# Expert stage of a fused encoder block: a third place for arriving weights, low parts only on VectorE, the last 16 tokens' gates on VectorE, gathers requested a step later

## Chip, core and metric

One core of a Trainium2 chip runs the whole program in one launch. The metric is the device time of that core in microseconds. The engines are TensorE (PE: matmuls, PEld: weight loads beside them), VectorE (DVE), ScalarE (ACT), GpSimd (Pool) and SyncE (SP, which here only issues DMAs). Each engine takes its instructions in program order, so one that waits holds all that stand behind it on its engine.

## What is computed

An encoder block over 512 tokens of width 2048: adaLN, neighbourhood attention and a bidirectional RWKV-7 mixer in parallel, an output projection, and then a product-key expert layer, which is where the change lies. Each token selects 16 of 16,384 single-neuron experts in each of 8 heads:

```
def chunk(args):
    xc, ec, gc = args
    hidden = jax.nn.gelu(jnp.einsum('cd,chkd->chk', xc, exp_u[ec]), approximate=False) * gc
    return jnp.einsum('chk,chkd->cd', hidden, exp_v[ec])
```

All of it is float32. A product x·w is made of three matmuls on parts: x and w are each split into a high part in a shorter format and a low part that holds the rest, and high·high, high·low and low·high are summed.

## The kernel before

The 512 tokens are handled in two ways. For the first 144 (TS) the rows of the selected experts are gathered: class Picks fetches, for one pick of 128 tokens, 128 rows of 8 KB by an indirect DMA that Pool issues (L1231), and DVE takes a dot product with it (L1253) or adds it, scaled, into y3 (L1264). k.rb = 3 row places go round. The other 368 tokens (TD) go through all experts densely, with a gate that is zero for experts that were not selected.

The dense part is class Experts. A unit "u" computes the hidden values of 128 experts for 368 tokens, a unit "v" adds 4 such experts' groups (512 experts) into 256 of the 2048 output columns. Each unit has two steps; a step needs one weight part of 128x1024 floats (512 KB, tile raw) and does 24 matmuls of 368 columns. There are 512 steps in all. form() runs the first 64 while the gates are still being made; main() runs the other 448, and is the stage "main" here. In the middle of main a round has 14 steps: 6 of "u" and 8 of "v".

The order in main is written out by hand, step by step (L1468 on). In step m: split(m+2) casts the weight part that arrived to its high part wh on ScalarE and makes the low part wl on DVE, or, in main with LPMAIN = 5, every fifth on Pool (w_split). load(m+4) requests the next part on SP, into the place that split(m+2) frees: k.rawb = 2 places go round. wh and wl have 3 places each. Then come the pieces kept in the list "late" from the step before, which split a group's hidden values into H (ScalarE copy L521, DVE subtraction L522); then step_done for the step that ended: for a "v", two additions into y on DVE (L1442); for a "u", Gelu on ScalarE (L1433) and gated(): Pool multiplies by the gates, 352 tokens at L1412 and the last 16 at L1415, and at the first of four groups SP requests the next gates (L1403, L1405) and a hidden tile that was put aside earlier (ge, L1420). Then the matmuls; six accumulators go round in "v", two a step. At the end of the step, if the pace says so, picks.step(): one dot or one addition of a gathered row on DVE, and behind it on Pool the request of the next gather into the row that becomes free. 24 steps before the end all picks are done.

Of the kernel before, what the change touches and what calls it, by code (L numbers as in the profile page):

```python
# [5 lines left out]
F32=mybir.dt.float32; F32R=mybir.dt.float32r; BF16=mybir.dt.bfloat16; I32=mybir.dt.int32; U32=mybir.dt.uint32  # L6
# [444 lines left out]
TD = 512 - TS  # L451
NB, HB = divmod(TD, 32)
# [751 lines left out]
class Picks:  # L1204
# [3 lines left out]

    def __init__(self, k):
        self.k, self.items, self.fetched, self.at = k, [], [], 0  # L1210
        for lo, hi in ((0, 128), (128, 128 + X2)):
            nb = (hi - lo) // self.BATCH
            for b in range(nb + 1):
                js = lambda i: [(i, lo + j) for j in range(self.BATCH * (b - i), self.BATCH * (b - i + 1))]
                dots, adds = js(0) if b < nb else [], js(1) if b else []
                mix = [x for p in zip(dots, adds) for x in p] if dots and adds else dots + adds
                self.items += mix
            self.items += [("x2", lo // 128), ("g2", lo // 128)]
# [16 lines left out]
    def step(self):  # L1235
        if self.at >= len(self.items):
            return
        k = self.k
        V, A, G = k.nc.vector, k.nc.scalar, k.nc.gpsimd
        while len(self.fetched) < k.rb:  # L1240
            self.fetch()
        kind, j = self.items[self.at]
        r = self.fetched[self.at]
        self.fetched[self.at] = None
        self.at += 1
        if kind == "x2":
            self.x2 = r
            return
        if kind == "g2":
            self.finish(j, r, self.x2)  # L1250
            self.fetch()
        elif kind == 0:
            V.scalar_tensor_tensor(r, r, 1.0, k.u3, ALU.mult, ALU.mult, accum_out=k.s3[:, j:j + 1])  # L1253
            if j % self.BATCH == self.BATCH - 1:
                cs = slice(j + 1 - self.BATCH, j + 1)
                A.activation(k.s3[:, cs], k.s3[:, cs], AF.Gelu)
                G.tensor_tensor(k.s3[:, cs], k.s3[:, cs], k.g3[:, cs], ALU.mult)  # L1257
            if j == 127:
                for a in range(128 // X2):
                    G.dma_start(k.u3[a * X2:(a + 1) * X2], k.u3b)  # L1260
        elif j % 128 == 0:
            V.tensor_scalar(k.y3, r, k.s3[:, j:j + 1], None, op0=ALU.mult)
        else:
            V.scalar_tensor_tensor(k.y3, r, k.s3[:, j:j + 1], k.y3, ALU.mult, ALU.add)  # L1264
        self.fetch()

    def finish(self, j, g2, x2):

# [42 lines left out]
                ex.main(pp, vp)  # L1311


LPMAIN = 5
NLEAD, NREST = 18, 3


class Experts:
# [16 lines left out]
    def load(self, m):  # L1335
        k = self.k
        if m < len(self.steps):
            kind, a, b, q = self.steps[m]
            self.raws[m] = k.W.tile([128, 1024], F32, name="raw", bufs=k.rawb)
            src = k.i["pv"][a, 2 * b + q] if kind == "v" else k.i["pu"][a, :, q * 1024:(q + 1) * 1024]  # L1340
            k.nc.sync.dma_start(self.raws[m], src)

# [12 lines left out]
    def form(self, gates):  # L1355
        k, tc = self.k, self.tc
        done, n = -1, 2 * NA
        with tc.high_priority():
            for m in range(k.rawb):
                self.load(m)  # L1360
            for m in range(2):
                self.split(m)
                self.load(m + k.rawb)
        acc = None
        for m in range(n):
            with tc.high_priority() if m < NLEAD else contextlib.nullcontext():
                k.lp = 2 if m + 2 < NLEAD else 3 if m + 2 < n - NREST else 0
                self.split(m + 2)
                self.load(m + 2 + k.rawb)
            if acc is not None and m % 2 == 0:  # L1370
                self.spill(m // 2 - 1, acc)
            if m % 2 == 0:
                acc = new_acc(k)
            self.rows_u(m, acc)
            while done < (gates.n + 1) * (m + 1 - NLEAD) // (n - NREST - NLEAD) and done < gates.n + 1:
                done += 1
                gates.step(done)
                if done % 2:
                    self.picks.step()
        self.spill(NA - 1, acc)  # L1380
        k.lp = 0
# [7 lines left out]
    def main(self, pp, vp):  # L1389
        k, gp, picks, steps, spilled, split, load, ws = self.k, self.gp, self.picks, self.steps, self.spilled, self.split, self.load, self.ws  # L1390
# [3 lines left out]
        ys = [vp.tile([128, TD], F32, name="y%d" % d) for d in range(16)]  # L1394
        hs, gts, ges, accs = {}, {}, {}, {}
        late = []
        picks.pp = pp

        def gates_of(g, by=nc.sync):
            if g < ng:  # L1400
                t = gts[g] = vp.tile([128, nb, 4, 32], F32, name="gt", bufs=2)
                src = k.G.rearrange("b p i t -> p b i t")[:, :, g * 4:(g + 1) * 4]
                by.dma_start(t[:, :NB].rearrange("p b c t -> p b (c t)"), src[:, :NB].rearrange("p b i t -> p b (i t)"))  # L1403
                if HB:
                    by.dma_start(t[:, NB, :, :HB], src[:, NB, :, :HB])  # L1405

        def gated(e):

            g, c = divmod(e, 4)
            ge = ges.pop(e)  # L1410
            gv = ge[:, :32 * NB].rearrange("p (b t) -> p b t", t=32)
            G.tensor_tensor(gv, gv, gts[g][:, :NB, c, :], ALU.mult)  # L1412
            if HB:
                gv = ge[:, 32 * NB:]
                G.tensor_tensor(gv, gv, gts[g][:, NB, c, :HB], ALU.mult)  # L1415
            if c == 0:
                gates_of(g + 1)
                if spilled(4 * g + 3):
                    ges[4 * g + 3] = gp.tile([128, TD], F32, name="ge", bufs=k.geb)
                    nc.sync.dma_start(ges[4 * g + 3], k.gel[g])  # L1420

            def parts():
                hs[e] = vp.tile([128, 2, TD], F32R, name="H", bufs=8)
                split_to(k, hs[e], ge)
            late.append(parts)
            if c == 2 and spilled(e + 1):
                gated(e + 1)

        def step_done(kind, a, b, q):
            if kind == "u":  # L1430
                if q:
                    ges[a] = gp.tile([128, TD], F32, name="ge", bufs=k.geb)
                    A.activation(ges[a], accs.pop("u")[:, :TD], AF.Gelu)  # L1433
                    gated(a)
                return
            for j, acc in enumerate(accs.pop(("v", q))):
                d = 4 * b + 2 * q + j
                y, acc = ys[d], acc[:, :TD]
                if a == 0:
                    V.tensor_copy(y, acc)  # L1440
                elif a < ng - 1:
                    V.tensor_tensor(y, y, acc, ALU.add)  # L1442
                else:
                    V.scalar_tensor_tensor(y, acc, k.mod[:, 80 + d:81 + d], y, ALU.mult, ALU.add)  # L1444
                    nc.sync.dma_start(k.o["outT"][d], y)
# [19 lines left out]
        first, early, todo = 2 * NA, picks.at, len(picks.items) - picks.at  # L1465
        pace = n - 24
        gates_of(0, nc.gpsimd)
        k.lp = LPMAIN  # L1468
        ended = None
        for m in range(first, n):  # L1470
            kind, a, b, q = steps[m]
            split(m + 2)
            load(m + 2 + k.rawb)
            for f in late:
                f()
            late.clear()
            done = ended
            if done:
                step_done(*done)
                if done[0] == "v" and done[1] == ng - 2:  # L1480
                    late.append(lambda d=done[2:]: finish_columns(*d))
            if m == n - 20:
                assert picks.at == len(picks.items)
                fetch_columns(0)
                fetch_columns(1)
            if kind == "u":
                if q == 0:
                    accs["u"] = new_acc(k)
                self.rows_u(m, accs["u"])
            else:  # L1490
                h, l = ws.pop(m)
                accs["v", q] = [pp.tile([128, 512], F32, name="acc5", bufs=6) for j in range(2)]
                for j, acc in enumerate(accs["v", q]):
                    for e in range(4):
                        w = slice(e * 256 + j * 128, e * 256 + j * 128 + 128)
                        mm3(k, acc, h[:, w], l[:, w], hs[4 * a + e], e == 0, e == 3, slice(0, TD))
            ended = steps[m]
            if picks.at < len(picks.items) and picks.at < early + todo * (m + 1 - first) // (pace - first):
                picks.step()
# [184 lines left out]
```

## Time and profile before

| | us |
|---|---|
| median of 3 runs | 4745.5 (4743.96 to 4752.61) |
| profiled execution | 4740.13 |
| its span | 4738.4 |
| main, first to last matmul | about 2680 to 4735 |
| busy over the whole span: TensorE / DVE / ACT / Pool | 4385.9 / 3314.8 / 1743.2 / 1894.1 |

The profile is of one execution. Busy time of TensorE includes its wait inside pipelined matmuls, so the number of matmuls in a stretch and the granted clock tell more than its busy share. "Idle before" names what ended the idle time of an engine ahead of an instruction.

### The profile page before, as it was taken

To read this page: it belongs to the slowest core of one execution; us is meant where nothing else is said; L and a number is where in the kernel's file an instruction comes from. 1 tells how busy PE (TensorE), PEld (TensorE's weight loads), DVE (VectorE), ACT (ScalarE), POOL (GpSimd) and SP (SyncE) were. 2 spreads that over 40 slices of the span, in tenths; PEclk is the share of its full clock that TensorE was granted. 3 is DMA by queue.
4 is the path that set the end of the run, shared out by engine and by line. 5 is a ranking of instruction groups with operands and counts; after the bars stand their busy time and mean duration, and the time that the engine had idled before them with its cause. 6 is when DMAs were issued, how large, how long until landed. Compare 5 with 4: busy or idle time off the path is not lost. (4 is left out here: it accounts for less than half of the span.)

```text
span 4738.4 us, 67546 instructions
## 1 busy us (share of the span) xinstructions
PE 4385.9 (93%) x25113; PEld 3880.1 (82%) x25113; DVE 3314.8 (70%) x4934; ACT 1743.2 (37%) x3352; POOL 1894.1 (40%) x1614
## 2 busy tenths in 40 slices
PE   6979999999998989989989989999898999998899
PEld 5757777777776878878889988999898998888889
DVE  8857666555553766649999677777777777776775
ACT  4532445444443433342356422222222222222222
POOL 4235444444332322432244434445343444443542
PEclk9989999999988989999999999999999999999999
DMA  9775444434334766732368877778777787778775
GB/s 329 246 238 150 123 117 129 122 107 118 107 89 133 231 205 200 276 103 91 104 227 286 276 264 278 282 275 292 260 281 267 278 288 279 280 266 271 265 271 172
DMA packets 391066, 1016.00 MB, mean 214 GB/s; under 512 B 100336, under 2 KB 152560, under 8 KB 351792
## 3 DMA queue, kind: packets, MB, share of 16 engines
q1 hardware_dynamic: 339312, 659.47, 43.3%
q0 software_dynamic: 51424, 352.21, 20.3%
q8 instruction: 198, 3.24, 0.3%
q14 instruction: 132, 1.08, 0.1%
HBM read 924.61 MB, written 86.91 MB: 213 GB/s over the span
## 5 line engine op out<-in xcount | busy, mean ns | idle before, releaser
L131 PE MATMUL acc<-X,wh 128*128 128x368 f32 (+1 forms) x7680 | 2231.8, 369 | 19.7 <-ACT wh L131 12.4
L131 PEld LDWEIGHTS acc<-X,wh 128*128 128x128 f32 x7680 | 1411.4, 191 | 167.1 <-ACT wh L131 14.4
L131 ACT CAST wh<-raw 128x1024 fp32r<-128x1024 f32 (+1 forms) x952 | 834.4, 879 | 1707.8 <-DMA raw<-pu 539.1
L131 PE MATMUL acc<-X,wl 128*128 128x368 f32 (+1 forms) x3840 | 1419.4, 370 | 44.1 <-POOL wl L131 36.1
L131 PE MATMUL acc<-H,wh 128*128 128x368 f32 x4096 | 1051.3, 339 | 85.1 <-DVE y L1442 82.8
L131 DVE TENSOR_TENSOR wl<-raw,wh 128x1024 fp32r<-128x1024 f32 (+1 forms) x555 | 706.4, 1274 | 574.2 <-ACT wh L131 563.4
L131 POOL TENSOR_TENSOR wl<-raw,wh 128x512 fp32r<-128x512 f32 (+1 forms) x397 | 703.6, 1774 | 850.7 <-ACT wh L131 766.4
L131 PEld LDWEIGHTS acc<-X,wl 128*128 128x128 f32 x3840 | 734.2, 191 | 131.9 <-POOL wl L131 45.9
L131 PEld LDWEIGHTS acc<-H,wh 128*128 128x128 f32 x4096 | 746.0, 193 | 99.2 <-issue 55.2
L131 PE MATMUL acc<-H,wl 128*128 128x368 f32 x2048 | 691.9, 338 | 52.3 <-POOL wl L131 49.5
L131 PEld LDWEIGHTS acc<-H,wl 128*128 128x128 f32 x2048 | 395.3, 193 | 63.9 <-POOL wl L131 59.4
L1231 POOL DMA_INDIRECT row<-un,idx x144 | 192.0, 1333 | 531.9 <-DVE y L1264 473.2
L1264 DVE SCALAR_TENSOR_TENSOR y<-row,s,y 128x2048 f32<-128x2048 f32 x142 | 365.0, 2570 | 0.0
L1253 DVE SCALAR_TENSOR_TENSOR row<-row,u 128x2048 f32<-128x2048 f32 x144 | 359.5, 2496 | 0.0
L1231 POOL DMA_INDIRECT row<-vn,idx x144 | 183.5, 1274 | 366.8 <-DVE row L1253 331.5
L1442 DVE TENSOR_TENSOR y<-y,acc 128x368 f32<-128x368 f32 x480 | 233.7, 531 | 0.0
L131 DVE SCALAR_TENSOR_TENSOR SVU<-us,Wc,S0w 64x64 f32<-64x64 f32 x224 | 63.4, 283 | 226.5 <-PE us L131 222.3
L1412 POOL TENSOR_TENSOR ge<-ge,gt 128x352 f32<-128x352 f32 x128 | 168.6, 1317 | 82.9 <-ACT ge L1433 66.5
L554 DVE SCALAR_TENSOR_TENSOR adacc<-adaw,sc,adacc 128x512 f32<-128x512 f32 x180 | 164.5, 914 | 43.5 <-DMA adaw<-ada 41.4
L522 DVE TENSOR_TENSOR H<-ge,H 128x368 fp32r<-128x368 f32 x128 | 120.8, 953 | 93.9 <-ACT H L521 93.9
L1157 DVE TENSOR_TENSOR o<-ct,selT 128x1024 f32<-128x1024 f32 x92 | 145.8, 1614 | 15.2 <-PE pg L1182 15.1
L131 DVE TENSOR_TENSOR M<-Q,MT 128x8 f32<-128x8 f32 (+14 forms) x240 | 122.7, 511 | 7.9
(329 smaller groups left out, 4814.5 us busy)
## 6 DMA issues: line engine op xcount, KB each, us to landing
raw<-pu SPq DMA_DIRECT2D x256, 512.0 KB
raw<-pv SPq DMA_DIRECT2D x256, 512.0 KB
adaw<-ada SPq DMA_DIRECT2D x192, 512.0 KB
raw<-w_in SPq DMA_DIRECT2D x272, 256.0 KB
G<-st POOLq DMA_DIRECT2D x11, 2048.0 KB, 8.2
gt<-G SPq DMA_DIRECT2D x31, 704.0 KB
raw<-w_ab SPq DMA_DIRECT2D x32, 512.0 KB
raw<-w_out SPq DMA_DIRECT2D x32, 512.0 KB
```

The source lines that it names most:

```text
L131: return f(*a, **kw)
L522: k.nc.vector.tensor_tensor(dst[:, 1], src, dst[:, 0].bitcast(F32), ALU.subtract)
L554: V.scalar_tensor_tensor(a, w[:, j], c, a, ALU.mult, ALU.add)
L1157: eng.tensor_tensor(o, in0, in1[:, t:t + 8].unsqueeze(2).to_broadcast([128, 8, 128]), op)
L1231: k.nc.gpsimd.indirect_dma_start(out=t, out_offset=None, in_=k.i[("un", "vn")[kind]], in_offset=bass.IndirectOffsetOnAxis(ap=k.idx3[:, j:j ...
L1253: V.scalar_tensor_tensor(r, r, 1.0, k.u3, ALU.mult, ALU.mult, accum_out=k.s3[:, j:j + 1])
L1264: V.scalar_tensor_tensor(k.y3, r, k.s3[:, j:j + 1], k.y3, ALU.mult, ALU.add)
L1412: G.tensor_tensor(gv, gv, gts[g][:, :NB, c, :], ALU.mult)
L1442: V.tensor_tensor(y, y, acc, ALU.add)
```

## The change

It touches class Picks and class Experts only.

- A third place for weight parts: every third load goes to a tile raw3 in another pool, and each load is requested one step earlier relative to its use (m+5 where m+4 stood), in form() and in main().
- LPMAIN is gone: in main all low parts are made on DVE. form() keeps its share on Pool.
- The gates of the last 16 tokens are multiplied on DVE, at the head of the late piece, instead of on Pool in gated(). The gate tile is laid out so that these 16 tokens lie by themselves.
- In main a gather isn't requested at once after the row was used, but in the next step, after step_done.

```diff
     def step(self):
+        self.pay()
...
-        self.fetch()
+        if not self.defer:
+            self.fetch()
+        else:
+            self.owed += 1
+
+    def pay(self):
+        while self.owed:
+            self.fetch()
+            self.owed -= 1
...
-LPMAIN = 5
...
-            self.raws[m] = k.W.tile([128, 1024], F32, name="raw", bufs=k.rawb)
+            pool, name, bufs = (k.W, "raw", k.rawb) if m % 3 < 2 else (self.gp, "raw3", 1)
+            self.raws[m] = pool.tile([128, 1024], F32, name=name, bufs=bufs)
...
-                self.load(m + 2 + k.rawb)
+                self.load(m + 5)
...
-                t = gts[g] = vp.tile([128, nb, 4, 32], F32, name="gt", bufs=2)
+                t = vp.tile([128, 4 * TD], F32, name="gt", bufs=2)
+                t = gts[g] = (t[:, :128 * NB].rearrange("p (b c t) -> p b c t", c=4, t=32), t[:, 128 * NB:].rearrange("p (c t) -> p c t", c=4))
...
-            G.tensor_tensor(gv, gv, gts[g][:, :NB, c, :], ALU.mult)
-            if HB:
-                gv = ge[:, 32 * NB:]
-                G.tensor_tensor(gv, gv, gts[g][:, NB, c, :HB], ALU.mult)
+            G.tensor_tensor(gv, gv, gts[g][0][:, :, c, :], ALU.mult)
+            gt = gts[g]
...
             def parts():
+                if HB:
+                    gv = ge[:, 32 * NB:]
+                    V.tensor_tensor(gv, gv, gt[1][:, c, :], ALU.mult)
                 hs[e] = vp.tile([128, 2, TD], F32R, name="H", bufs=8)
                 split_to(k, hs[e], ge)
...
-        k.lp = LPMAIN
+        k.lp = 0
...
-            load(m + 2 + k.rawb)
+            load(m + 5)
...
                 step_done(*done)
+            picks.pay()
+            if done:
```

## Rows read from the trace of the kernel before

**Rows 1.** Windows: stretch, length, busy of each engine (count), clock, DMA share, GB/s.
```profile
2420.00:2680.00 260.00, 254.32 (x1757) 252.79 (x1756) 229.14 (x153) 176.20 (x421) 111.57 (x82) 1.00 0.81 287
...
2680.00:4738.00 2058.00, 1881.74 (x10761) 1839.34 (x10759) 1497.25 (x1412) 562.63 (x705) 882.59 (x662) 0.97 0.77 269
...
2680.00:2740.00 60.00, 52.71 (x289) 52.10 (x288) 32.78 (x24) 16.58 (x24) 32.49 (x26) 0.91 0.83 260
...
4637.00:4735.00 98.00, 97.62 (x578) 96.60 (x576) 53.95 (x76) 26.05 (x31) 25.21 (x18) 1.00 0.52 171
```

**Rows 2.** Waits in main: waiting engine and line, awaited: us, times, longest.
```profile
ACT wh L131 <- DMA raw<-pv: 532.8, 156, 8.9
...
DVE wl L131 <- ACT wh L131: 452.3, 220, 8.2
...
PE acc L131 <- DVE y L1442: 82.8, 30, 7.2
PE acc L131 <- POOL wl L131: 81.2, 53, 12.7
```

**Rows 3.** Timeline of SP, ACT and DVE, 3036 to 3050 us: start, length, instruction.
```profile
3036.76 4.57 SPq L1341 DMA_DIRECT2D raw<-pu  x2
3044.65 0.33 SPq L1341 DMA_DIRECT2D raw<-pv  x1
...
3042.30 1.06 ACT L131 CAST wh<-raw 128x1024 fp32r<-128x1024 f32 x1 [2.94 <-DMA raw<-pu]
...
3036.64 0.98 DVE L1442 TENSOR_TENSOR y<-y,acc 128x368 f32<-128x368 f32 x2
...
3040.89 2.35 DVE L1264 SCALAR_TENSOR_TENSOR y<-row,s,y 128x2048 f32<-128x2048 f32 x1
3043.39 1.23 DVE L131 TENSOR_TENSOR wl<-raw,wh 128x1024 fp32r<-128x1024 f32 x1 [0.16 <-ACT wh L131]
```

**Rows 4.** Timeline of SP, 3607 to 3640 us.
```profile
3625.86 3.60 SPq L1420 DMA_DIRECT2D ge<-gel  x1
```

**Rows 5.** DMA view of main: GB/s in 40 slices, packets, and issue to landing.
```profile
GB/s 249 274 265 258 291 275 264 296 287 285 287 281 274 262 275 252 297 276 253 287 266 285 295 290 285 281 258 277 284 277 272 256 273 249 274 280 274 243 169 177
DMA packets 172795, 552.41 MB, mean 269 GB/s; under 512 B 29324, under 2 KB 81036, under 8 KB 138461
...
row<-un,idx POOLq DMA_INDIRECT x129, 7.5
```

**Rows 6.** Groups in main, shapes apart: count | busy us, mean ns | idle before.
```profile
L131 DVE TENSOR_TENSOR wl<-raw,wh 128x1024 fp32r<-128x1024 f32 x358 | 497.8, 1391 | 461.0 <-ACT wh L131 452.3 <-PE acc L131 8.2
...
L1264 DVE SCALAR_TENSOR_TENSOR y<-row,s,y 128x2048 f32<-128x2048 f32 x133 | 343.9, 2586 | 0.0
...
L131 POOL TENSOR_TENSOR wl<-raw,wh 128x1024 fp32r<-128x1024 f32 x89 | 228.7, 2570 | 102.9 <-ACT wh L131 98.3 <-PE acc L131 3.5
L1412 POOL TENSOR_TENSOR ge<-ge,gt 128x352 f32<-128x352 f32 x128 | 168.6, 1317 | 82.9 <-ACT ge L1433 66.5 <-issue 12.8 <-DMA gt<-G 2.5
L1231 POOL DMA_INDIRECT row<-un,idx x129 | 168.3, 1305 | 462.0 <-DVE y L1264 427.7 <-issue 11.0 <-ACT wh L131 5.7
...
L1415 POOL TENSOR_TENSOR ge<-ge,gt 128x16 f32<-128x16 f32 x128 | 121.3, 948 | 0.0
L522 DVE TENSOR_TENSOR H<-ge,H 128x368 fp32r<-128x368 f32 x128 | 120.8, 953 | 93.9 <-ACT H L521 93.9
```

**Rows 7.** Groups of the whole span, shapes apart: a small DVE operation.
```profile
L131 DVE TENSOR_SCALAR a<-pm 128x8 f32<-128x8 f32 x16 | 2.7, 166 | 16.8 <-PE pm L131 16.6
```

**Rows 8.** Timeline of DVE at 3620 us: H with nothing beside it.
```profile
3620.04 0.54 DVE L522 TENSOR_TENSOR H<-ge,H 128x368 fp32r<-128x368 f32 x1 [0.64 <-ACT H L521]
```

**Rows 9.** Timelines of Pool and DVE, 4360 to 4400 us.
```profile
4386.43 4.63 POOL L1272 TENSOR_TENSOR row<-y,row 128x2048 f32<-128x2048 f32 x1
...
4387.04 4.43 DVE L522 TENSOR_TENSOR H<-ge,H 128x368 fp32r<-128x368 f32 x1 [0.65 <-ACT H L521]
4391.39 6.60 DVE L1253 SCALAR_TENSOR_TENSOR row<-row,u 128x2048 f32<-128x2048 f32 x1
```

More of the change, by code (lines that the diff above doesn't have):

```diff
@@ L1210, in __init__ @@
         self.k, self.items, self.fetched, self.at = k, [], [], 0
+        self.defer, self.owed = False, 0
         for lo, hi in ((0, 128), (128, 128 + X2)):
@@ L1358, in form @@
         with tc.high_priority():
-            for m in range(k.rawb):
+            for m in range(3):
                 self.load(m)
@@ L1362, in form @@
                 self.split(m)
-                self.load(m + k.rawb)
+                self.load(m + 3)
         acc = None
@@ L1396, in main @@
         late = []
-        picks.pp = pp
+        picks.pp, picks.defer = pp, True
         def gates_of(g, by=nc.sync):
             if g < ng:
-                t = gts[g] = vp.tile([128, nb, 4, 32], F32, name="gt", bufs=2)
+                t = vp.tile([128, 4 * TD], F32, name="gt", bufs=2)
+                t = gts[g] = (t[:, :128 * NB].rearrange("p (b c t) -> p b c t", c=4, t=32), t[:, 128 * NB:].rearrange("p (c t) -> p c t", c=4))
                 src = k.G.rearrange("b p i t -> p b i t")[:, :, g * 4:(g + 1) * 4]
-                by.dma_start(t[:, :NB].rearrange("p b c t -> p b (c t)"), src[:, :NB].rearrange("p b i t -> p b (i t)"))
+                by.dma_start(t[0].rearrange("p b c t -> p b (c t)"), src[:, :NB].rearrange("p b i t -> p b (i t)"))
                 if HB:
-                    by.dma_start(t[:, NB, :, :HB], src[:, NB, :, :HB])
+                    by.dma_start(t[1], src[:, NB, :, :HB])
         def gated(e):
```

## Prediction

> **What bounds the kernel now.** I read the windows view first, cut at the stage that the change touches. Main runs from about 2680 us to the last matmul at 4735 us, 2055 us of the span. TensorE is not held by its own work there: the last 98 us hold 578 matmuls at full clock, 0.170 us each [rows 1]. A step is 24 matmuls, so 4.07 us undisturbed; main's 448 steps are 10,752 matmuls, which at 98/578 us is 1823 us. So 2055 - 1823 = 232 us are lost: to idle time, and to the half clock that goes with it. The mean clock is 0.97 [rows 1], so 6% of 2058 us, 123 us, ran at 1.2 instead of 2.4 GHz and lost half of itself, 62 us; the other 170 us are idle time.
>
> The view of waits tells who ended that idle time: y <- y, acc on DVE 82.8 us in 30 waits, wl made by Pool 81.2 us in 53 [rows 2]. Behind these stands one cause. The longest waits of the stage are ScalarE's for a weight part to land, 532.8 us in 156 casts for parts of "v" alone; next come DVE's 452.3 us for such a cast [rows 2]. The timeline shows the loop: a load is issued at 3036.76, its cast starts at 3042.30, ended by the DMA, the low part starts at 3043.39 and takes 1.23, and the place is requested again at 3044.65 [rows 3]. That is 7.89 us for a place that serves every second step, against 8.14 us of matmuls; on the mean it is 2 x 2055/448 = 9.17 us. **Two places going round is the bound**; what it delays stands in order on DVE, ScalarE and Pool and reaches TensorE by whichever of them has least room.
>
> **The change, part by part.**
>
> *Third place.* Load m+5 goes out where load m+4 did, after split m+2, and has three steps to come round: 12.2 us instead of 8.1. The mean loop of 9.17 us, with all its present waits, then has 3 us to spare, and the three wh and wl let the casts stay two steps ahead of TensorE. A late case: once in a group of 14 steps SP has gate loads and a spilled ge to issue, the ge alone 3.60 us, with the next weight load behind it [rows 4]; such a slip is now covered by the spare. The same edit in the stage before main is costed at nothing: TensorE is busy 254 of 260 us there [rows 1] (bounds 0 and -5 us). What the transfers then need: 552.4 MB [rows 5] at a share of 0.77 of the 16 engines [rows 1]; in 1874 us (below) that is 295 GB/s and a share of 0.84. The best slices now carry 295 to 297, at eight or nine tenths busy [rows 5], so this fits, but not by much.
>
> *No low parts on Pool.* Removed: 89 of 2.57 us each on Pool [rows 6]; added: 89 on DVE of 1.23 us (the undisturbed one of [rows 3]), 109 us. Gone with them is the 81.2 us wait: a Pool low part stands behind a gather that waits for DVE to free its row (427.7 us of Pool's idle time before the gathers of un alone [rows 6]).
>
> *Last 16 tokens.* Removed: 128 on Pool, 0.95 us each, 121.3 us [rows 6]. Added: 128 on DVE over 128x16; the nearest rows are a one-input 128x8 at 0.166 us [rows 7] and the two-input 128x368 of H at 0.54 us [rows 8]; I take the middle, 0.35 us, since the second input costs something and 16 columns little: 45 us (21 to 69). A new wait comes with it: ScalarE's copy of H now waits for DVE's gate, and DVE then for that copy, 0.64 us even where nothing else is in the way [rows 8]: 128 x 0.64 = 82 us, about the 93.9 us that DVE waits there today [rows 6]. Behind the copy on ScalarE stands the next cast, which the three wh hold until TensorE has ended a step anyway, so that is hidden unless DVE is over 2 us behind.
>
> *Less of Pool beside DVE.* DVE's work on two inputs stretches beside Pool's tensor work: a low part takes 1.391 us on the mean instead of 1.23, y3 2.586 instead of 2.35, H 0.953 instead of 0.54 [rows 3, 6, 8]. By their counts 58 + 31 + 53 us, and the 130 dots, taken as stretched like y3, 30: 172 us. Pool's tensor work falls from 229 + 169 + 121 = 519 us [rows 6] to some 145 (128 of about 0.95 to 1.32 us), and the stretch in proportion to 48 us: -124 us. The Trainium skill (SBUF — State Buffer, "Who interferes with whom") has the two engines share one port pair under an exclusive lock, the loser blocked for the whole instruction; an H of 4.43 us beside a Pool operation of 4.63 us agrees [rows 9], the mean low part, which loses only 0.16 us, doesn't show it.
>
> *DVE's sum.* 1497 [rows 1] + 109 + 45 - 124 = 1527 us busy (upper end 1497 + 109 + 69 = 1675), with H's waits 1609 (1757), against 1823 us of matmuls: 3.6 us of a 4.07 us step. The heaviest step: cast 1.06, low 1.23 [rows 3], gate, copy and H 0.35 + 0.64 + 0.54, two y adds 0.98, one row 2.35 [rows 3]: 7.1 us. The accumulators (6, two a step) must be free 8.14 us after the step began. It fits, with 1 us to spare.
>
> *Gathers a step later.* The gather still waits for the row that DVE frees; what changes is that it stands behind the next step's gate on Pool instead of ahead of it. 261 picks in 424 steps are one in 1.62 steps, so three rows are 4.9 steps, 20 us; a landing takes 7.5 us [rows 5], and DVE's idle time before y3's additions is 0.0 [rows 6]. A step (4 us) fits; cost 0, and without that cover what lies over 20 us, at most 4 us a pick.
>
> *Gate buffers.* SP's load of the next gates now also waits for DVE's gate of the group before, with weight loads queued behind it; that gate is issued two steps earlier, so 0 (bound: SP's hold-up of today again, 3.60 us in 14 steps, inside the spare).
>
> **The sum.** Main: 1823 us. The head, where 289 matmuls take 60 us instead of 49 [rows 1], keeps 8 (5 to 11). The finish of the first 128 tokens, untouched, has two such Pool operations in a row, with DVE held in H and a dot for 4.43 and 6.60 us [rows 9]: 10 (0 to 22, the upper end with its half clock). Other lateness of DVE keeps 20 of the 164 us of waits for y and Pool's wl (0 to 80). The half clock after what is left is 62 x 38/170 = 13 (5 to 35). Total 1874, so -181 us: the profiled execution (4740.1 us, 1.7 us around its span) goes to 4559 us. The median of the three runs is 5.4 us higher, 4745.5; less 181 it is 4564. I say **4562 us**.
>
> **The rivals.**
>
> (a) *DVE becomes the bound.* If three quarters of its 452 us of waits for casts stay in its queue: 1527 + 82 + 339 = 1948 us, -107, 4636 us. For it: DVE runs in order and gains 217 instructions. Against: those waits are for weight parts that now come earlier. Chance 0.10. The Trainium skill (Perfetto Trace Analysis, "Optimizing Scalar/DVE Operations") would take work off a saturated DVE, even to GpSimd, with the reserve that the two share a port; this change does the reverse, and by that advice this rival would be likelier; the row has DVE at 1497 of 2058 us, not saturated [rows 1].
>
> (b) *Transfers are the bound.* A third outstanding load only lengthens each. At the 280 GB/s of the stage's ordinary slices [rows 5] main takes 552.4/0.280 = 1973 us, -82, 4661 us; at 295 GB/s no more than the forecast. Chance 0.09.
>
> (c) *The third place does nothing*, because SP holds the loads [rows 4] either way: only the Pool wait goes, 81 us and its share of the clock, 62 x 81/170 = 30: -111, 4632 us. Chance 0.06.
>
> (d) *No change*: transfers lengthen until the loop takes three of today's mean steps, 13.8 us: 4743 us. Chance 0.03.
>
> (e) *Slower.* The landings come no earlier and the 154 us of new DVE work lie behind each late cast, while Pool's 81 us go: +73 us, 4816 us. It decides when DVE's work and waits in a round of 14 steps exceed today's 64.2 us (2055/32). Chance 0.06.
>
> **How the numbers follow.** The forecast (4505 to 4610) has 0.66, the rivals what stands with them. The low end of the range has all residues at their lower ends: 1823 + 10 = 1833, -222, 4523; less 5 for the stage before main, and 13 for a step of 4.04 us, should the last 98 us themselves not be undisturbed (an allowance of mine): 4505. The upper end takes in the upper residues in part and (a) and (c): 4650. Outside lie (b), (d) and (e). A measurement of this kernel tells 0.2% (9.5 us) from no change. Faster 0.91, same 0.03, slower 0.06.
>
> **What would show it.** After: some 1150 matmuls in each 200 us of main; ScalarE's waits for raw<-pv well under half of 532.8 us, its waits for TensorE in their place; no wait of TensorE for Pool; DVE near 1527 us busy with low parts near 1.27 us; three places going round in 9 to 12 us. Wrong: TensorE waiting over 60 us for DVE's wl or y (a); weight loads that take over 7 us to land (b); SP holding loads (c); DVE idle before rows, that is, a gather that came late.

## The result, and the profile after

The changed kernel takes 4517.0 us (4515.58 to 4526.64, 3 runs) against 4745.5: ratio 0.9521, 95% interval 0.9495 to 0.9546, 228.5 us less. It is faster, as forecast, inside the range, and 45 us better than the 4562 us that were said. The span of the profiled execution is 4513.8 us; main runs from its first matmul at 2681 us to the last at 4510 us, 1829 us instead of 2055. The span is 224.6 us shorter, so all of it is main's (226 us); TensorE in the stage before it is busy 254.44 of 260 us, as in [rows 1]. Within main, TensorE's idle time fell from 173 to 14 us, and its time at half clock from 123 to 14 us, half of which is lost: 158 and 55, together 213 of the 226 us.

Windows of the changed kernel; the columns are those of [rows 1]: stretch, length, busy time and count of PE, PEld, DVE, ACT and Pool, then clock, DMA share and GB/s.
```profile
2420.00:2680.00 260.00, 254.44 (x1748) 252.92 (x1747) 229.29 (x153) 176.84 (x421) 113.03 (x82) 0.99 0.80 286
2680.00:2740.00 60.00, 54.52 (x314) 53.60 (x313) 37.98 (x36) 17.32 (x25) 28.09 (x19) 0.97 0.86 275
2680.00:4510.00 1830.00, 1815.59 (x10767) 1809.33 (x10765) 1515.17 (x1627) 565.76 (x704) 673.38 (x445) 1.00 0.84 302
...
3000.00:3200.00 200.00, 200.00 (x1195) 200.00 (x1194) 171.97 (x185) 63.51 (x81) 80.91 (x51) 1.00 0.87 314
```
From 3000 to 3600 us TensorE works through three stretches of 200 us without a gap, 1195 matmuls in each, 0.1674 us apiece, with the full clock granted. DVE's busy time has hardly changed (1497 us in [rows 1]), but it now falls into 1830 us.

Waits in main of the changed kernel, answering to [rows 2] (us, times, longest).
```profile
ACT wh L131 <- PE acc L131: 659.4, 265, 6.7
...
DVE wl L131 <- ACT wh L131: 214.0, 183, 3.8
...
ACT wh L131 <- DMA raw<-pv: 104.7, 47, 4.2
...
DVE H L522 <- ACT H L521: 76.3, 123, 0.6
ACT wh L131 <- DMA raw<-pu: 60.1, 18, 5.2
...
PE acc L131 <- DVE wl L131: 8.9, 4, 2.8
PE acc L131 <- DVE y L1456: 3.0, 3, 2.4
```
Two more of these waits in the kernel before:
```profile
ACT wh L131 <- DMA raw<-pu: 483.7, 152, 7.5
...
ACT wh L131 <- PE acc L131: 132.8, 42, 6.4
```
This is the sign to look for: the cast that used to wait for the DMA (533 and 484 us) now waits for TensorE, 659 us instead of 133, that is for a wh to come free. The stage has turned from waiting for its input to being ahead of it. TensorE itself waits 14 us in all.

Timelines of ScalarE and DVE of the changed kernel at 3043 us, answering to [rows 3].
```profile
3043.47 1.05 ACT L131 CAST wh<-raw 128x1024 fp32r<-128x1024 f32 x1 [2.99 <-PE acc L131]
3047.48 1.05 ACT L131 CAST wh<-raw 128x1024 fp32r<-128x1024 f32 x1 [2.96 <-PE acc L131]
...
3044.76 1.22 DVE L131 TENSOR_TENSOR wl<-raw,wh 128x1024 fp32r<-128x1024 f32 x1
```
Casts follow one another every 4.01 us, each started by TensorE.

Groups in main of the changed kernel, answering to [rows 6] (count | busy us, mean ns | idle before).
```profile
L131 DVE TENSOR_TENSOR wl<-raw,wh 128x1024 fp32r<-128x1024 f32 x446 | 587.8, 1320 | 210.3 <-ACT wh L131 206.9 <-ACT s L1258 2.4
...
L1266 DVE SCALAR_TENSOR_TENSOR y<-row,s,y 128x2048 f32<-128x2048 f32 x133 | 328.8, 2472 | 2.3 <-DMA row<-vn,idx 2.3
L1255 DVE SCALAR_TENSOR_TENSOR row<-row,u 128x2048 f32<-128x2048 f32 x130 | 311.6, 2397 | 4.7 <-DMA row<-un,idx 4.7
...
L1425 POOL TENSOR_TENSOR ge<-ge,gt 128x352 f32<-128x352 f32 x128 | 229.9, 1806 | 253.9 <-ACT ge L1447 173.1 <-issue 80.8
...
L522 DVE TENSOR_TENSOR H<-ge,H 128x368 fp32r<-128x368 f32 x128 | 69.5, 543 | 81.2 <-ACT H L521 76.3 <-issue 4.9
...
L1436 DVE TENSOR_TENSOR ge<-ge,gt 128x16 f32<-128x16 f32 x128 | 26.6, 207 | 8.6 <-DMA gt<-G 8.6
```
DMA view of main after, answering to [rows 5].
```profile
GB/s 268 328 314 317 302 300 323 323 310 310 305 300 338 296 324 288 338 316 315 312 312 284 341 315 310 310 304 303 336 311 310 304 292 279 324 309 302 250 177 166
DMA packets 172658, 552.00 MB, mean 302 GB/s; under 512 B 29295, under 2 KB 80995, under 8 KB 138324
```
The same bytes at 302 GB/s on the mean; single slices reach 341, more than any slice of before.

### The profile page after: what moved, and what is told of

Its sections match the earlier page's. It is cut to its first block, busy times and chain, and to the rows that moved or that the text cites. A ratio compares the mean times of both kernels' runs of the same rounds, so it can differ in the third digit from the quotient of the medians.

```text
span 4513.8 us, 67464 instructions
## 1 busy us (share of the span) xinstructions
PE 4321.4 (96%) x25113; PEld 3852.0 (85%) x25113; DVE 3333.8 (74%) x5151; ACT 1746.5 (39%) x3352; POOL 1688.9 (37%) x1397
## 4 chain that ended last, share of the span: by engine, by line
PE 75%; DVE 9%; DMA 4%; issue 3%; POOL 2%; ACT 1%; SPq 0%; POOLq 0%; ACTq 0%; DVEq 0%
PE acc L131 65%; PE pm L131 4%; PE us L131 2%; PE xo L131 2%; PE pg L1182 1%; DVE wl L131 1%; DMA adaw<-ada 1%; DMA TT<-sQ 1%; DVE ix L1091 1%; DMA raw<-w_in 1%; DVE pos L1103 1%; DVE v L1090 1%; DVE ts L1102 0%; SPq L131 0%; DVE cand L1098 0%
## 5 line engine op out<-in xcount | busy, mean ns | idle before, releaser
L131 DVE TENSOR_TENSOR wl<-raw,wh 128x1024 fp32r<-128x1024 f32 (+1 forms) x644 | 801.0, 1246 | 323.9 <-ACT wh L131 316.3
L131 PE MATMUL acc<-H,wh 128*128 128x368 f32 x4096 | 1026.9, 332 | 4.0 <-DVE y L1456 3.0
L131 POOL TENSOR_TENSOR wl<-raw,wh 128x512 fp32r<-128x512 f32 (+1 forms) x308 | 478.3, 1555 | 732.7 <-ACT wh L131 659.6
L131 PEld LDWEIGHTS acc<-H,wh 128*128 128x128 f32 x4096 | 730.5, 189 | 5.4 <-ACT wh L131 3.9
L1232 POOL DMA_INDIRECT row<-un,idx x144 | 230.2, 1598 | 453.2 <-DVE y L1266 400.9
L1255 DVE SCALAR_TENSOR_TENSOR row<-row,u 128x2048 f32<-128x2048 f32 x144 | 343.5, 2386 | 4.7 <-DMA row<-un,idx 4.7
L1232 POOL DMA_INDIRECT row<-vn,idx x144 | 220.3, 1530 | 305.3 <-DVE row L1255 274.6
L1425 POOL TENSOR_TENSOR ge<-ge,gt 128x352 f32<-128x352 f32 x128 | 229.9, 1806 | 253.9 <-ACT ge L1447 173.1
L521 ACT CAST H<-ge 128x368 fp32r<-128x368 f32 x128 | 64.0, 500 | 267.5 <-DVE ge L1436 261.2
L522 DVE TENSOR_TENSOR H<-ge,H 128x368 fp32r<-128x368 f32 x128 | 69.5, 543 | 81.2 <-ACT H L521 76.3
```

The costliest lines, as they stand in the source:

```text
L131: return f(*a, **kw)
L521: k.nc.scalar.copy(dst[:, 0], src)
L522: k.nc.vector.tensor_tensor(dst[:, 1], src, dst[:, 0].bitcast(F32), ALU.subtract)
L1232: k.nc.gpsimd.indirect_dma_start(out=t, out_offset=None, in_=k.i[("un", "vn")[kind]], in_offset=bass.IndirectOffsetOnAxis(ap=k.idx3[:, j:j ...
L1425: G.tensor_tensor(gv, gv, gts[g][0][:, :, c, :], ALU.mult)
```

## Experiments

The theory after the result (the loop theory): with two places, the round of a weight part through its place (request, landing, cast, low part, next request) was longer than the two steps of matmuls (2 x 24 x 0.1674 = 8.04 us) that it serves, and the third place alone lifts that. The 9.17 us of the prediction are two mean steps of main, which is the time from request to request whatever holds it up. What fills them can be added up from the trace of the kernel before, over 435 rounds of main (a landing is the last of the 128 packets of 4 KB of a part, taken in order of time): request to landing 4.5 us, landing to cast 0.95, cast 1.05, cast to low part 0.9, low part 1.6, to the next request 0.2. Hardly any of it is a part that lies and waits. In the changed kernel a part that has landed lies 3.8 us on the mean before its cast.

The rivals of this theory: Pool's low parts behind the gathers were the cause; Pool's tensor work beside DVE was; the edits need each other; or the third place helps by something other than the loop. All ratios are to the kernel before on the same chip.

**One part undone at a time.** Two places again, in form() too, the other three edits kept:

```diff
-            pool, name, bufs = (k.W, "raw", k.rawb) if m % 3 < 2 else (self.gp, "raw3", 1)
-            self.raws[m] = pool.tile([128, 1024], F32, name=name, bufs=bufs)
+            self.raws[m] = k.W.tile([128, 1024], F32, name="raw", bufs=k.rawb)
...
-            load(m + 5)
+            load(m + 2 + k.rawb)
```


> The changed kernel with two places for weight parts again, loads requested at m+4; the other three edits stay. Loop theory (the round of two places was the bound): ScalarE waits for raw<-pv several hundred us again (104.7 us in the changed kernel, 532.8 before), and the time goes back to 4632 to 4720 us, of the gain of 228.5 us only what Pool's 81 us and their half clock were worth stays. Pool theory (Pool's low parts behind gathers were the cause, the late loads only showed it): below 4560 us.

Measured: 4741.2 us, ratio 0.9978 (0.9964 to 0.9993). Main took 2055 us, exactly what it took before. Both expectations missed: the time goes back further than the loop theory had priced. TensorE's idle time in main is 166 us (173 before), and its time at half clock, 171 us, is longer than the 123 of before. Waits in the run with two places:
```profile
ACT wh L131 <- DMA raw<-pv: 463.3, 131, 11.9
...
ACT wh L131 <- DMA raw<-pu: 438.5, 141, 9.7
...
PE acc L131 <- DVE y L1455: 114.4, 33, 7.6
PE acc L131 <- DVE wl L131: 33.3, 32, 2.6
PE acc L131 <- ACT wh L131: 10.0, 8, 4.3
```
Pool's 81.2 us of [rows 2] are gone, as they must be, and the time with them is not: y has 114.4 instead of 82.8 us, DVE's wl 33.3 and the cast 10.0. Whoever delivers last is named, but the lateness is that of the loads.

Every fifth low part on Pool again, the rest as changed:

```diff
-        k.lp = 0
+        k.lp = 5
```


> The changed kernel with every fifth low part of main on Pool again; third place, gates and gathers as changed. Loop theory: with parts landing early the Pool low part has room, its 2.57 us hide, 4517 to 4545 us and waits of TensorE for Pool's wl under 20 us. Pool theory: the 81 us of waits for Pool's wl and their 30 us of half clock come back, 4590 to 4630 us.

Measured: 4524.05 us, ratio 0.9531 (0.9515 to 0.9547). TensorE's waits for Pool's wl:
```profile
PE acc L131 <- POOL wl L131: 16.1, 6, 6.9
```
16 us instead of 81, as the loop theory has it. Low parts on Pool are harmless once the loads are early. Here the gathers are still requested a step later; the run with the third place alone, below, has Pool's old order whole.

The last 16 tokens on Pool again:

```diff
             G.tensor_tensor(gv, gv, gts[g][0][:, :, c, :], ALU.mult)
+            if HB:
+                gv = ge[:, 32 * NB:]
+                G.tensor_tensor(gv, gv, gts[g][1][:, c, :], ALU.mult)
...
-                if HB:
-                    gv = ge[:, 32 * NB:]
-                    V.tensor_tensor(gv, gv, gt[1][:, c, :], ALU.mult)
```


> The changed kernel with the last 16 tokens' gates on Pool again. Loop theory: 4512 to 4530 us, nothing on the path. Stretch theory (Pool's tensor work beside DVE is what made DVE late): 121 us of Pool's work come back, DVE busy rises by some 30 us, waits of TensorE for DVE come back in part, 4535 to 4570 us.

Measured: 4523.33 us, ratio 0.9524 (0.9506 to 0.9542): nothing that can be told from the changed kernel. DVE's busy time from 2680 to 4510 us did not rise, as the stretch theory has it, but is 1490 us instead of 1515: the 27 us of these gates have left it.

Gathers requested at once again:

```diff
-        picks.pp, picks.defer = pp, True
+        picks.pp, picks.defer = pp, False
```


> The changed kernel with each gather requested at once after the row was used. Loop theory: 4512 to 4530 us; DVE doesn't wait for rows in either. Queue theory (the gather ahead of the gate on Pool makes H late and DVE with it): waits of ScalarE for the gates rise and TensorE waits for y again, 4540 to 4600 us.

Measured: 4519.21 us, ratio 0.9523 (0.9492 to 0.9553): nothing either.

**The third place alone.** All three undone together, in the changed kernel's gate layout:

```diff
-        k.lp = 0
+        k.lp = 5
...
-        picks.pp, picks.defer = pp, True
+        picks.pp, picks.defer = pp, False
...
+                G.tensor_tensor(gv, gv, gts[g][1][:, c, :], ALU.mult)
...
-                    V.tensor_tensor(gv, gv, gt[1][:, c, :], ALU.mult)
```


> The kernel before with the third place for weight parts alone (and the gate tile's new layout, which it needs room for): Pool makes every fifth low part and the last 16 tokens' gates, gathers are requested at once. Loop theory: 4515 to 4545 us, the whole gain but what the Pool low parts cost. Theory that the edits need each other (Pool's order, low part behind gather behind DVE, takes over as the bound once loads are early): 4570 to 4640 us, with some 80 us of waits of TensorE for Pool's wl left.

Measured: 4528.05 us, ratio 0.9515 (0.9486 to 0.9544), against the whole change's 0.9521. Main took 1841 us in its profiled execution, 12 more than the changed kernel's. Its waits of TensorE:
```profile
PE acc L131 <- POOL wl L131: 18.7, 9, 8.3
PE acc L131 <- DVE y L1456: 5.0, 5, 1.8
```
One edit of the four has the gain. The other three together are worth 0 to 12 us, less than these runs can tell; without the third place they were worth 0.2%. Pool's old order, low parts behind gathers that are requested at once, now costs TensorE 18.7 us of waits, not some 80: the edits don't need each other.

**Is it the loop, or only one place more?** Here all three places stay, but each is held one step longer by a copy of one column behind the next low part, so that a load goes out where it went out with two places (self.old is the weight part of the step before):

```diff
...
             split(m + 2)
+            if m + 2 < n:
+                V.tensor_copy(hold, self.old[:, :1])
             load(m + 5)
```


> The changed kernel, all three places there, but in each step of main a copy of one column on DVE reads the weight part of the step before, behind the next low part. A place comes free a step later and the next load goes out where it went out with two places; nothing else moves. Loop theory: two steps of matmuls (8.1 us) again against a loop of 9 us, main near 2055 us, 4690 to 4780 us. If the third place helps by something else (more transfers under way on SP's queue, another stretch of memory): as the run with the same copies that hold nothing, 4517 to 4550 us.

The same copies from a tile that nobody waits for, as the price of the instructions:

```diff
+                V.tensor_copy(hold, k.mod[:, :1])
```


> The changed kernel with the same 448 copies of one column on DVE, from a tile that nobody waits for: the price of these instructions alone. By DVE's room (138 us more cost some 46 us in the run with every fourth low part twice) 448 of 0.06 to 0.17 us, 27 to 76 us, cost 0 to 25 us: 4517 to 4545 us.

And the holding copy on ScalarE, behind the next cast, which leaves DVE out of the loop:

```diff
+                A.copy(hold, self.old[:, :1])
```


> The changed kernel with the copy of one column on ScalarE, behind the next cast: a place comes free when the cast of the next part is done, a step later than without it, but DVE's low part and what stands ahead of it on DVE are out of the loop. Loop theory: issue to landing 5.4 us, to the cast 0.5, the cast 1.05, about 7 to 8 us against 8.1: main loses only where a landing is late, 4540 to 4640 us, clearly below the run that holds on DVE. If the number of free places alone counts: as that run, 4690 us or more.

Measured: 4703.96 us (ratio 0.9912, 0.9887 to 0.9938) held on DVE, 4513.91 us (0.9514, 0.9499 to 0.953) with the same copies that hold nothing, 4559.8 us (0.9596, 0.957 to 0.9623) held on ScalarE. Waits of ScalarE for weight parts, held on DVE:
```profile
ACT wh L131 <- DMA raw<-pu: 461.0, 143, 8.1
...
ACT wh L131 <- DMA raw<-pv: 426.5, 156, 8.0
```
and held on ScalarE:
```profile
ACT wh L131 <- DMA raw<-pu: 341.6, 94, 8.1
...
ACT wh L131 <- DMA raw<-pv: 257.0, 102, 9.8
```
The copies on DVE cost nothing (the time is even 3 us below what was expected); holding the place costs 190 us. In the trace, the place is requested again 4.7 us after its own low part ended when it is held on DVE, 2.2 us when held on ScalarE, 0.2 in the changed kernel. With three places present, a request that is a step late brings back five sixths of the loss, and taking DVE's queue out of the hold takes most of it away again. So the length of the round counts, not the number of tiles. With two places and no low part on Pool, DVE's share in the round (0.8 us from cast to low part and 1.3 for the low part, of 9.2) is what lifts it above 8.04 us; the largest share is the 4.7 us to the landing. There is no run with copies on ScalarE that hold nothing, so part of the 46 us held there may be their own price. Held on DVE main is 2019 us, not near 2055 as expected, and the run is still some 30 us below the one with two places, with the request behind the same low part; why, these runs don't show.

**How much room does DVE have?** Every fourth, then every second low part of main computed twice (k.twice is 4, then 2):

```diff
+    if getattr(k, "twice", 0) and k.nsplit % k.twice == 0:
+        k.V.tensor_tensor(l, raw, h.bitcast(F32), ALU.subtract)
...
```


> The changed kernel with every fourth low part of main computed twice on DVE, 112 more of 1.23 us, 138 us of DVE work that nothing needs. If DVE has the room that its busy time shows (1515 us of 1830, with 138 more and 76 us of waits for H's copy 1729): 4517 to 4540 us. If DVE in its order is already close to the bound: 4575 us or more.

> The changed kernel with every second low part of main computed twice on DVE, 224 more of 1.23 us, 275 us. DVE then has 1790 us of work and 76 us of waits for H's copy, 1866 us against main's 1829: 4550 to 4620 us by its busy time, and TensorE waits for DVE. If DVE is already close to the bound: over 4700 us, nearly all 275 us on the path.

Measured: 4568.43 us (0.9605, 0.9576 to 0.9633) and 4670.32 us (0.9819, 0.9791 to 0.9848); in the traces main is 46 and 154 us longer than the changed kernel's. Windows of main and waits of TensorE, every fourth:
```profile
2690.00:4500.00 1810.00, 1764.68 (x10374) 1744.91 (x10373) 1612.45 (x1670) 542.95 (x687) 696.71 (x445) 0.99 0.84 299
...
PE acc L131 <- DVE y L1458: 27.3, 26, 2.5
PE acc L131 <- DVE wl L131: 12.9, 10, 2.4
```
and every second:
```profile
2690.00:4500.00 1810.00, 1697.61 (x9781) 1660.49 (x9780) 1655.98 (x1690) 507.53 (x647) 658.35 (x420) 0.98 0.80 285
...
PE acc L131 <- DVE y L1458: 54.5, 46, 3.4
PE acc L131 <- DVE wl L131: 53.3, 51, 4.1
...
DVE wl L131 <- ACT wh L131: 86.5, 82, 3.3
DVE H L524 <- ACT H L523: 79.7, 128, 0.9
```
Both came out between their expectations: of the first 138 us a third lies on the path, of the next 137 us four fifths (108). DVE reaches 1656 of 1810 us, 91%, and no more in these runs; over all of main it still waits 80 us for H's copy and 87 us for casts. The changed kernel, at 1515 of 1830 us, stands, by what did not come onto the path (138 - 46 and 275 - 154), some 90 to 120 us below the point from which DVE decides. That is an estimate: the second low part reads the weight part and writes wl again, so it also holds the place and TensorE's operand 1.2 us longer, and these runs don't part the two.

**A better finish?** The two long Pool operations after the first 128 tokens cut into four column pieces each:

```diff
-            G.tensor_tensor(g2, k.y3, g2, ALU.mult)
-            G.tensor_tensor(x2, x2, g2, ALU.add)
+            for c in range(4):
+                cs = slice(c * 512, (c + 1) * 512)
+                G.tensor_tensor(g2[:, cs], k.y3[:, cs], g2[:, cs], ALU.mult)
+                G.tensor_tensor(x2[:, cs], x2[:, cs], g2[:, cs], ALU.add)
```


> The changed kernel with the finish of the first 128 tokens on Pool in four column pieces of 512 instead of two operations of 4.6 us over 2048 columns. If what holds DVE there is each long Pool operation as a whole, the waits of TensorE near 4200 us in the span shrink by 5 to 8 us and with their half clock 6 to 12 us are gained: 4505 to 4511 us. If the sum of Pool's time counts, not its pieces: 4515 to 4520 us.

Measured: 4518.99 us, ratio 0.9494 (0.9469 to 0.9519): no gain that can be told, as for Pool's total counting. In the trace the eight pieces take 14.4 us of Pool where the two operations took 10.1, and TensorE's waits from 4100 to 4300 us are 15 us where they were 9: they did not shrink. The intervals of this and the changed kernel overlap, and the two medians are 2 us apart. No kernel here clearly beats the changed one.

## Why the prediction was right, step by step

*The bound* was read right: the round of the two places. The runs with two places, with a third, and with a third that is held show it. The one round that was read, 7.89 us, would have fitted two steps, though; that rounds are longer on the mean stood on main's length alone, and the sum of the rounds above bears it out.

*The sum* gave main 1874 us, 1829 were measured. Two terms were too large. The step without disturbance was taken as 4.07 us, from a stretch of 98 us in [rows 1]; the run without gaps shows 0.1674 x 24 = 4.02 us, so 10,752 matmuls take 1800 instead of 1823 us, 23 of the 45 us. The residues (head 8, finish 10, lateness of DVE 20, half clock 13) were 51; they are 29: TensorE's gaps in main sum to 14 us, and 14 us ran at half clock, which costs 7; the other 8 are in neither (eight wider matmuls of the second finish, at 4409 us, take 3 of them). The lateness of DVE, put at 20, is the 8.9 + 3.0 us above. The head is there (314 matmuls in the first 60 us instead of the 358 that fit, 7 us), and the finish: the next rows show it. There is luck in the range: without its allowance of 13 us for a shorter step, and 5 for the stage before main, which did not come, the low end would have been 4523 us, 6 above the measured time. The allowance named the right term.

Timelines of Pool and DVE of the changed kernel at the finish, answering to [rows 9].
```profile
4186.64 4.63 POOL L1283 TENSOR_TENSOR row<-y,row 128x2048 f32<-128x2048 f32 x1
4191.34 5.50 POOL L1284 TENSOR_TENSOR row<-row 128x2048 f32<-128x2048 f32 x1
...
4187.74 4.61 DVE L131 TENSOR_TENSOR wl<-raw,wh 128x1024 fp32r<-128x1024 f32 x1 [2.78 <-ACT wh L131]
4192.27 4.60 DVE L1436 TENSOR_TENSOR ge<-ge,gt 128x16 f32<-128x16 f32 x1
```
A gate that takes 0.207 us on the mean took 4.60 here, beside Pool's operation of 5.50, and a low part 4.61 beside the one of 4.63.

*DVE's sum* held: 1527 us said, 1515 measured. The gate of 16 tokens was 0.207 us, near the lower end (0.17 to 0.54); H beside less of Pool's work is at its undisturbed 0.543; the low part at 1.320, above the 1.27 said. H's waits for the copy were 76 us in 123 waits of at most 0.6 us, where 82 were said. Terms that were off in opposite ways helped: the gates took 18 us less than said, while Pool's gate over 352 tokens took 230 us where some 145 were said for all its tensor work, and the stretch that stayed on low parts, y3 and dots is some 70 us (by 1.23, 2.35 and 2.29 us undisturbed) instead of 48.

*Pool's low parts* were mis-sized, though it didn't show in the total: the prediction let their 81.2 us leave by themselves and built rival (c), 4632 us, on it. With two places and no low part on Pool the time was 4741 us. A wait that stands at the end of a chain is not a cost of its own; it was counted as one.

*Gathers a step later* and *gate buffers* cost nothing, as said: DVE waits 2.3 + 4.7 us for rows in all of main.

*Rivals.* (b), transfers: excluded by the 302 GB/s, of which no slice of [rows 5] had given a sign. The prediction had taken 295 to 297 as nearly the most; it was only what was asked for. Its mechanism is there in part: with three places a part lands 5.2 us after its request instead of 4.5, and one in ten takes over 7 us, but a part then lies 3.8 us before its cast. (a), DVE: not here, but 90 to 120 us away, as the doubled low parts show. (c) and (d) are excluded by the run with the third place alone. (e) would have needed parts that are ready no earlier; they are ready earlier. By the Trainium skill (Perfetto Trace Analysis, "Optimizing Scalar/DVE Operations") moving work off DVE to GpSimd may pay where DVE is saturated; at 1515 of 1830 us it wasn't, and the run with Pool's low parts back gains nothing.

## What to carry to other kernels

Where a consumer waits for a load again and again, write down the whole round of one place, from request over landing and every engine that must have read it to the next request, and divide by the places: if that is more than the step, it is the bound, whatever engine the final wait names. Take the parts of the round at their mean, not at their best (here 9.15 against 7.89 us), and leave out the time that a part only lies ready. A place that a busy in-order engine must release is held for that engine's queue too, so count its lateness in. Then ask which waits would be gone by themselves: here the 81 us on Pool and the 83 us on DVE were the same lateness, and removing the one without the round only handed it to the other.

## What the runs showed of the hardware

The Trainium skill (Trainium Kernel Development and Optimization, "Best Practices") advises to double-buffer. Here two places ran at 9.17 us per two steps, against a round that can take 7.89 us [rows 3] and 8.04 us of matmuls, and main was 226 us longer than with a third. Landings took 3.0 to 6.3 us from the request in eight of ten loads before: a round that fits only when it is short has nothing to catch up with after a late one. Transfers went at up to 341 GB/s in a slice of 46 us of main with 552 MB to move, while the same bytes had shown at most 297 with two places. Pool's work is longer beside DVE's, not only the other way: the gate over 352 tokens took 1.806 us on the mean, 1.317 in [rows 6], and a gather's request 1.586 instead of 1.305. With hardly any of DVE's two-input work on SBUF tiles beside it a gate took 0.94 us in both kernels, otherwise 1.47 before and 1.90 after; 37 of 128 were free of it before, 13 after. How busy DVE is doesn't decide it: with two places and the other three edits, DVE is busy 74% of main, as before (73%), and the gate took 1.792. What runs beside the gate tells more.
